# Seven half-size products for the left half of the output projection, with the weight sums made during the input projection

## The chip, the cores and the metric

The kernel runs on one core of a Trainium2 chip. The metric is the time in device microseconds, as the median of the runs. A profile shows five engines: PE (matrix multiplication, with its weight loads as PEld), DVE (vector), ACT (scalar, activations), POOL (here an issuer of transfers and some element work) and SP (an issuer of transfers).

## What is computed

One encoder layer for 512 positions and a width of 2048, everything in 32-bit floats. Cut to what matters:

```
h = x @ w_in                       # (512,2048) @ (2048,8192)
qa,ka,va,ga,qb,kb,vb,gb = split(h) # eight blocks of 1024 columns
ya = dilated_attention(qa,ka,va)   * silu(ga)      # 16 heads, group A
yb = neighbourhood_attention(qb,kb,vb) * silu(gb)  # 16 heads, group B
out = concat(ya, yb) @ w_out       # (512,2048) @ (2048,2048)
result = layer_norm(alpha * x + out, gain, bias)
```

Every matrix product is made three times over: each operand is split into a high part that is rounded to the matmul's format and a low part that is the rest, and the product is high x high + low x high + high x low. The high part is an ACT copy, the low part a DVE subtraction, so each weight tile of 128 x 1024 costs one ACT and one DVE instruction before PE can use all of it.

## The kernel before

The program has four stages.

*Early block* (`plain_block`, L268): the first four of sixteen gate column tiles, while x is loaded and its sums are formed.

*Projection blocks* (`strassen_block`, L351, run by `run_blocks`, L491). Six blocks (k, q and v of each group) and, after the fourth, one block for the next six gate column tiles (`MID`), are each made as seven products of half-size matrices instead of eight (Strassen's scheme in a form with few sums). A block is a row of *jobs*; a job is one weight tile, twelve 512-wide matmuls (L405 to L407; L395 to L397 for the gates, 256 wide). For each job there are up to four steps: DVE adds two weight tiles (L373), ACT rounds (L377), DVE subtracts (L382), PE multiplies. `run_blocks` writes out the order by hand: at position n it adds for job n+3, rounds for n+2, does what is queued "behind" n (evictions, loads, sums of results), subtracts for n+2 and multiplies for n. PE, DVE and ACT keep this order.

```
if 0 <= n + 3 < len(jobs): jobs[n + 3][0]()       # add (DVE)
if split_: h = jobs[n + 2][1]()                   # high (ACT)
for fn in behind.pop(n, ()): fn()                 # what was put behind n
if split_: ready.append(jobs[n + 2][2](h))        # low (DVE)
if 0 <= n < len(jobs): jobs[n][3](*ready.pop(0))  # matmuls (PE)
```

POOL meanwhile writes the attention bias tables to memory: `prep_heads` (L156) for the sixteen heads of group A, eight loads and one store a head (L161, L163) through the buffers b0 and b1 in turn, then `prep_b` (L165 on) for group B through the same two. Its order is left to a scheduler, but everything on POOL runs one after the other.

*Attention* (the loop at L845, 136 steps of 128 queries of one head, eight steps a pair of heads). Each step has scores (L677, L678), a minimum on DVE (L634), an exponential on ACT (L638), two steps later transposes on PE (L697), and every fourth step the product with v (L719). Between them `fill` issues matmuls of two kinds: the remaining six gate tiles (`gate_unit`, L566, 48 wide matmuls each), then the first half of K of the output projection (`out_first`, L788). How many are issued per step is a table (`amount`). The order is written out for PE, SP, DVE and ACT. `share` (L725) sends the softmax denominators out and back in rows through POOL; `gated` (L744) divides and splits y into halves as `yk`.

*Output.* For all four column blocks of 512 the second half of K is multiplied (L778); column blocks 0 and 1 first, then for each of the four row blocks of 128 the column blocks 2 and 3. alpha x is added (`residual`, L911), `finish` adds the sums and takes statistics, `norm` (L919) normalises a row block and writes it out; in two row blocks it uses ACT and POOL for one quarter. The last row block has its own `last_norm`, in which PE makes the shift rows.

Of the kernel before, what the change touches and what calls it, by code (L numbers as in the profile page):

```python
# [65 lines left out]
EARLY, MID = 4, 6  # L66
# [5 lines left out]
def hybrid_layer(tc, xT, xn, w_in, w_early, w_mid, w_gate, w_out, t5x, brow, rpb, cmask, eye, gain, lbias, out):  # L72
    nc = tc.nc
    from contextlib import ExitStack
    with ExitStack() as ctx:
# [59 lines left out]
        sg_d = dram.tile([2 * PAIRS, 128, S], F32, name="sg_d")  # L135
        rc_d = dram.tile([2 * PAIRS, 8, 128], F32, name="rc_d")
# [214 lines left out]
        def strassen_block(src, kind, g, hooks):  # L351

            base = len(jobs)
            units, tiles = 4, 2
            cols, wide = (128 * MID // 2, (512, HALF * (MID // 2 - 2))) if kind == "s" else (512, (512, 512))

            def load(q, tags):
                def run():
                    for u in range(units):
                        raw = slot(tags[u], F32, "braw")[:, :2 * cols]  # L360
# [6 lines left out]
            def product(i, pool, q, other=None, onto=None):  # L367
# [7 lines left out]
                def high(u):  # L375
                    h = halves.next("wh", F32R)[:, :2 * cols]
                    nc.scalar.activation(h, raws[q][u], AF.Copy)  # L377
                    return h

                def low(u, h):  # L380
                    l = halves.next("wl", F32R)[:, :2 * cols]
                    nc.vector.tensor_tensor(l, raws[q][u], f(h), ALU.subtract)  # L382
                    return h, l

                def run(u, h, l):
                    if u == 0 and first:
                        accs.extend(bank(pool, "acc")[:, :n] for n in wide)
                    if kind == "s":
                        for kk in range(2):
                            k = 2 * u + kk  # L390
                            ah, al = operand(i, k)
                            for n in range(MID // 2):
                                c = slice(cols * kk + 128 * n, cols * kk + 128 * n + 128)
                                o = accs[n // 2][:, HALF * (n % 2):HALF * (n % 2) + HALF]
                                nc.tensor.matmul(o, h[:, c], ah, start=first and k == 0 and n % 2 == 0, stop=False, skip_group_check=skip)  # L395
                                nc.tensor.matmul(o, h[:, c], al, start=False, stop=False, skip_group_check=skip)  # L396
                                nc.tensor.matmul(o, l[:, c], ah, start=False, stop=k == 7 and (n % 2 == 1 or n == MID // 2 - 1),  # L397
                                                 skip_group_check=skip)
# [25 lines left out]
            def pair(name):  # L424
                if name not in made:
                    t = temps.next(name)
                    made[name] = [t[:, :512], t[:, 512:512 + wide[1]]]
# [10 lines left out]
            for q, ahead, i in ((0, 6, 0), (1, 4, 1), (3, 2, 2)):  # L438
                behind.setdefault(base - ahead if base else -4, []).append(load(q, tags[i]))
            at(2, 2, load(2, tags[1]))  # L440
# [30 lines left out]
            def put(name, ch, half, t):  # L471
# [4 lines left out]
                sg = vst.next("sg")[:, :wide[t]]  # L476
                silu(sg, o)
                for n in range(wide[t] // HALF):
                    nc.sync.dma_start(sg_d[EARLY + MID // 2 * ch + 2 * t + n][:, HALF * half:HALF * half + HALF], sg[:, HALF * n:HALF * n + HALF])
# [44 lines left out]
        stream = [w_gate[i] for i in range(2 * (2 * PAIRS - EARLY - MID))] + [w_out[8 * dc + u] for dc in range(4) for u in range(4)]  # L524
# [10 lines left out]
        def prepare():  # L535
# [8 lines left out]
            if not raws:  # L544
                return
            raw = raws.pop(0)
# [197 lines left out]
        def gated(i):  # L744

            y = yt[i]
            t = slot(y_tags[i], F32R, "yk").rearrange("p (s q) -> p s q", s=2)
            yk.append(t)

            def divide():  # L750
                nc.vector.tensor_tensor(y, y, rcs[i], ALU.mult)
                later(0, high)

            def high():
                nc.scalar.activation(t[:, 0], y, AF.Copy, scale=0.5)
                hold(2, low)

            def low():
                nc.vector.scalar_tensor_tensor(t[:, 1], y, 0.5, f(t[:, 0]), op0=ALU.mult, op1=ALU.subtract)
# [8 lines left out]
        def out_load(ring, dc, u):  # L768
            return load_split(ring, w_out[dc * 8 + u])

        def out_mms(acc, t, u, wh, wl, first, last, part=slice(0, 512)):
            c = slice(t * 128, t * 128 + 128)
            for kk in range(2):
# [3 lines left out]
                for n, (s, w) in enumerate(((0, wh), (1, wh), (0, wl))):  # L777
                    nc.tensor.matmul(acc[:, part], yk[k][:, s, c], w[:, wk], start=first and kk == 0 and n == 0,  # L778
# [3 lines left out]
        def keep(t, to, acc):  # L782
            if t % 2:
                nc.vector.tensor_copy(to, acc)
            else:
                nc.scalar.activation(to, acc, AF.Copy)

        def out_first(dc):  # L788

            if dc % 2 == 0:  # L790
                for t in range(4):
                    z[t].append(slot(f"x{6 + 2 * t + dc // 2}", F32, f"z{t}").rearrange("p (s q) -> p s q", s=2))
            accs = []
            for u in range(4):
                wh, wl = next_weight()
                for t in range(4):
# [3 lines left out]
                    if u == 3:  # L800
                        later(0, lambda t=t: keep(t, z[t][dc // 2][:, dc % 2], accs[t]))

        def fillers():
            for j in range(EARLY + MID, 2 * PAIRS):
                yield from gate_unit(j)
            z.extend([] for _ in range(4))
            for dc in range(4):
# [17 lines left out]
        def close():  # L825

            for fn, dve in tasks.pop(step[0], ()):
                if dve and 0 <= step[0] < 134:
# [5 lines left out]
        load_kq(0)  # L834
        load_bias(0)
        load_v(0)
        engines = {mybir.EngineType.PE, mybir.EngineType.SP, mybir.EngineType.DVE, mybir.EngineType.Activation}
        with tc.manual_schedule(engines=engines):
            prepare()
            for _ in range(3):  # L840
                close()
            while step[0] < 0:
                fill(7)
                close()
            for n in range(136):  # L845
# [12 lines left out]
                if mixing:  # L858
                    if exponent:
                        exponent()  # L860
                    behind_min(2)
                    fill(2)
                    mine, theirs, y, t = values(n // 4 - 1)
                    nc.scalar.activation(t, theirs, AF.Copy)
                    nc.vector.tensor_tensor(y, mine, t, ALU.add)
                    fill(amount - 2)
                else:
                    fill(2)
                if 2 <= n < 130:
                    turn(n - 2)  # L870
                if b == 3 or n >= 134:
                    behind_min(99 if n >= 134 else 2 if len(held) > 3 and held[0][0] > 1 else 1)
# [6 lines left out]
                if n >= 8 and n % 8 == 1:  # L879
# [8 lines left out]
            for n in (0, 400):  # L888
                fill(n)
                while tasks or held:  # L890
                    behind_min(99)
                    close()
        z = [[zt[i // 2][:, i % 2] for i in range(4)] for zt in z]

        gb, bb = [], []
        for tiles, src, first in ((gb, gain, 0), (bb, lbias, 6)):
            for i in range(4):
                t = slot(f"n{first + i}", F32, "gain")
                nc.sync.dma_start(t, _view(src, 512 * i, [[0, 128], [1, 512]]))
                tiles.append(t)  # L900

        xl = {}

        def load_x(i):
            for t in range(4):
                if t % 2 == 0:
                    two = slot(f"s{t // 2}", F32, "xl").rearrange("p (t q) -> p t q", t=2)
                xl[t, i] = two[:, t % 2]
# [222 lines left out]
```

## Time and profile before

| what | value |
|---|---|
| median of the runs | 973.45 us (lowest 973.0) |
| the profiled execution | 973.54 us, span 971.8 us, granted clock 0.998 |
| PE busy | 963.0 us, 4861 matmuls |
| DVE busy | 768.5 us |
| ACT busy | 501.3 us |
| POOL busy | 181.6 us |
| moved | 194.18 MB, mean 200 GB/s |

The span is the time from the first to the last instruction of one profiled execution; the time of a run has a little more around it. The first job of the projection blocks starts at 50.0 us, the first scores at 595.9, the last product of the output ends near 962.6. A line of a timeline gives start and duration in us, the engine, the line of the kernel, the operation, what it writes and reads, and in brackets how long the engine stood idle before it and what ended that.

### The profile page before, as it was taken

To read this page: it belongs to the slowest core of one execution; us is meant where nothing else is said; L and a number is where in the kernel's file an instruction comes from. 1 tells how busy PE (TensorE), PEld (TensorE's weight loads), DVE (VectorE), ACT (ScalarE), POOL (GpSimd) and SP (SyncE) were. 2 spreads that over 40 slices of the span, in tenths; PEclk is the share of its full clock that TensorE was granted. 3 is DMA by queue.
4 is the path that set the end of the run, shared out by engine and by line. 5 is a ranking of instruction groups with operands and counts; after the bars stand their busy time and mean duration, and the time that the engine had idled before them with its cause. 6 is when DMAs were issued, how large, how long until landed. Compare 5 with 4: busy or idle time off the path is not lost.

```text
span 971.8 us, 14211 instructions
## 1 busy us (share of the span) xinstructions
PE 963.0 (99%) x4861; PEld 804.6 (83%) x4861; DVE 768.5 (79%) x1169; ACT 501.3 (52%) x870; POOL 181.6 (19%) x321
## 2 busy tenths in 40 slices
PE   8999999999999999999999999999999999999997
PEld 6878888888888889998888888888888888888886
DVE  7897778679789778789679875788877777777877
ACT  7454444444444344454445544777777776763300
POOL 1006646735645000000000000111111010010020
PEclk9999999999999999999999999999999999999999
DMA  9715797698496086272196178777787667678213
GB/s 331 283 65 133 224 332 213 169 313 219 115 348 200 37 255 159 74 278 92 44 294 180 48 227 279 245 228 246 242 276 221 214 210 228 197 238 287 73 58 116
DMA packets 121255, 194.18 MB, mean 200 GB/s; under 512 B 49551, under 2 KB 70415, under 8 KB 121184
## 3 DMA queue, kind: packets, MB, share of 16 engines
q1 hardware_dynamic: 108672, 170.21, 54.8%
q0 software_dynamic: 11936, 22.42, 8.3%
q8 instruction: 38, 0.62, 0.3%
q10 hardware_dynamic: 576, 0.66, 0.2%
q14 instruction: 33, 0.27, 0.1%
HBM read 148.69 MB, written 44.50 MB: 199 GB/s over the span
## 4 chain that ended last, share of the span: by engine, by line
PE 97%; DMA 1%; DVE 1%; ACT 0%; issue 0%; SPq 0%; DVEq 0%; ACTq 0%
PE acc L405 16%; PE acc L407 16%; PE acc L406 16%; PE acc L778 16%; PE acc L572 6%; PE pv L719 4%; PE pt L697 4%; PE sc L678 2%; PE sc L677 2%; PE acc L397 2%; PE acc L396 2%; PE acc L395 2%; PE pt L260 1%; PE acc L279 1%; PE sc L778 1%; PE acc L280 1%
## 5 line engine op out<-in xcount | busy, mean ns | idle before, releaser
L377 ACT ACTIVATE wh<-braw 128x1024 fp32r<-128x1024 f32 (+1 forms) x196 | 202.1, 1031 | 277.3 <-PE acc L406 202.4
L382 DVE TENSOR_TENSOR wl<-braw,wh 128x1024 fp32r<-128x1024 f32 (+1 forms) x196 | 234.3, 1197 | 57.9 <-ACT wh L377 57.6
L405 PE MATMUL acc<-wh,xk 128*128 128x512 f32 x384 | 151.3, 394 | 0.0
L407 PE MATMUL acc<-wl,xk 128*128 128x512 f32 x384 | 149.7, 390 | 0.0
L406 PE MATMUL acc<-wh,xk 128*128 128x512 f32 x384 | 149.5, 389 | 0.0
L373 DVE TENSOR_TENSOR braw<-braw 128x1024 f32<-128x1024 f32 (+1 forms) x112 | 132.4, 1182 | 0.0
L778 PE MATMUL acc<-wh,yk 128*128 128x512 f32 x320 | 113.5, 407 | 0.0
L405 PE MATMUL acc<-wh,op 128*128 128x512 f32 x288 | 113.1, 393 | 0.0
L407 PE MATMUL acc<-wl,op 128*128 128x512 f32 x288 | 112.2, 390 | 0.0
L406 PE MATMUL acc<-wh,op 128*128 128x512 f32 x288 | 112.1, 389 | 0.0
L703 DVE TENSOR_TENSOR tl<-pt,th 128x256 fp32r<-128x256 f32 (+1 forms) x128 | 71.1, 556 | 30.3 <-ACT th L702 28.5
L407 PEld LDWEIGHTS acc<-wl,xk 128*128 128x128 f32 x384 | 72.1, 188 | 15.3
L405 PEld LDWEIGHTS acc<-wh,xk 128*128 128x128 f32 x384 | 72.1, 188 | 15.2 <-ACT bias L151 0.9
L406 PEld LDWEIGHTS acc<-wh,xk 128*128 128x128 f32 x384 | 72.2, 188 | 14.4
L638 ACT ACTIVATE p<-s,mn 128x512 f32<-128x512 f32 (+1 forms) x96 | 62.4, 650 | 30.6 <-DVE mn L634 29.9
L634 DVE CUSTOM_DVE_ANT_0 s<-sc,biases 128x512 f32<-128x512 f32 (+2 forms) x128 | 67.6, 528 | 11.4 <-PE sc L678 11.0
L702 ACT ACTIVATE th<-pt 128x256 fp32r<-128x256 f32 (+1 forms) x128 | 62.2, 486 | 23.0 <-PE pt L697 21.3
L778 PEld LDWEIGHTS acc<-wh,yk 128*128 128x128 f32 x320 | 58.1, 189 | 8.4 <-ACT wh L88 0.4
L161 POOL DMA_DIRECT2D bias<-rows_d x128 | 61.4, 487 | 16.1 <-DMA rows_d<-bias 5.2
L407 PEld LDWEIGHTS acc<-wl,op 128*128 128x128 f32 x288 | 54.1, 188 | 11.4
L406 PEld LDWEIGHTS acc<-wh,op 128*128 128x128 f32 x288 | 54.1, 188 | 10.9
L405 PEld LDWEIGHTS acc<-wh,op 128*128 128x128 f32 x288 | 54.1, 188 | 10.9
(188 smaller groups left out, 1774.6 us busy)
## 6 DMA issues: line engine op xcount, KB each, us to landing
braw<-in_w_in SPq DMA_DIRECT2D x96, 512.0 KB
wraw<-in_w_out SPq DMA_DIRECT2D x32, 512.0 KB
k_d<-kst SPq DMA_DIRECT2D x64, 128.0 KB
q_d<-kst SPq DMA_DIRECT2D x64, 128.0 KB
v_d<-vst SPq DMA_DIRECT2D x32, 256.0 KB
q<-q_d SPq DMA_DIRECT2D x32, 256.0 KB
k<-k_d SPq DMA_DIRECT2D x16, 512.0 KB
braw<-in_w_mid SPq DMA_DIRECT2D x16, 384.0 KB
```

What stands on the lines that cost most here:

```text
L161: nc.gpsimd.dma_start(bt[16 * r:16 * r + 16], _view(rows_d, h * 16 * ROW + 463 - 64 * r, [[ROW - 1, 16], [1, 560]]))
L373: nc.vector.tensor_tensor(raws[q][u], raws[q][u], raws[other][u], ALU.add)
L377: nc.scalar.activation(h, raws[q][u], AF.Copy)
L382: nc.vector.tensor_tensor(l, raws[q][u], f(h), ALU.subtract)
L405: nc.tensor.matmul(accs[t], ah[:, q], h[:, c], start=first and k == 0, stop=False, skip_group_check=skip)
L406: nc.tensor.matmul(accs[t], al[:, q], h[:, c], start=False, stop=False, skip_group_check=skip)
L407: nc.tensor.matmul(accs[t], ah[:, q], l[:, c], start=False, stop=k == 7, skip_group_check=skip)
L634: nc.vector.tensor_tensor_reduce(*flat, bias, 1.0, 3e38, ALU.add, ALU.min, mn)
L638: nc.scalar.activation(p[:, to:to + n].rearrange("p (b r c) -> p b r c", r=8, c=c), s[:, :n].rearrange(order, r=8, c=c), AF.Exp, bias=mn, ...
L702: nc.scalar.activation(th, pt[:, :nch], AF.Copy)
L703: nc.vector.tensor_tensor(tl, pt[:, :nch], f(th), ALU.subtract)
L778: nc.tensor.matmul(acc[:, part], yk[k][:, s, c], w[:, wk], start=first and kk == 0 and n == 0, stop=last and kk == 1 and n == 2)
```

## The change

- `MID` is 4 instead of 6. The gate block has two tiles a side, so 14 jobs of 24 matmuls of 256 columns instead of 28 of 18, and two more `gate_unit`s run in attention.
- The left half of the output's columns (column blocks 0 and 1) is made by seven half-size products over all of K, after attention. The right half stays as it was: column blocks 2 and 3, first half of K in attention, second half after it, column block 2 for all rows (`second_half`) and column block 3 row block by row block (`third`, and the tail).
- The products need sums of weights: four sums for each of eight column strips. `sum_weights` makes them in the projection blocks: POOL loads four tiles of 128 x 512 into b0 and b1, DVE adds four times (L522), POOL stores each sum to `t_d`. It is placed behind the jobs 30, 39, 48, 142, 152, 162, 172 and 182, the additions four to seven positions later.
- They also need sums of y. POOL stores each y to `y_d` in attention (L784); after attention `again` loads it back, `combine_y` makes the sums, `high_y` and `low_y` split them.
- Results of column blocks 2 and 3 are added to alpha x as they are evicted (L811), x being loaded in attention. POOL's order is written out in attention too. The table of `amount` is ((4,5,3,5) if n < 80 else (4,4,3,4)) in place of ((3,5,3,5) if n < 76 else (5,6,4,6)), the loop has 132 steps, `share` comes one step later.
- The jobs after attention are run by `project`, with its order written out as in the blocks. `norm` is on DVE and one small ACT instruction alone.

The diff, cut to its core:

```diff
-EARLY, MID = 4, 6
+EARLY, MID = 4, 4
...
+        def sum_weights(n, u, kk):
+
+            c, two = slice(512 * kk, 512 * kk + 512), []
+
+            def load():
+                two.extend(slot(f"b{m}", F32, "wsum")[:, :1024].rearrange("p (s q) -> p s q", s=2) for m in range(2))
+                for m, q in enumerate((0, 8, 12, 4)):
+                    nc.gpsimd.dma_start(two[m // 2][:, m % 2], w_out[q + u][:, c])
+
+            def put(m):
+                a, b = two
+                o, p = ((a[:, 0], a[:, 1]), (a[:, 1], b[:, 0]), (b[:, 0], a[:, 0]), (b[:, 1], b[:, 0]))[m]
+                nc.vector.tensor_tensor(o, o, p, ALU.add)
+                nc.gpsimd.dma_start(t_d[m][u][:, c], o)
+
+            behind.setdefault(n, []).append(load)
+            for m in range(4):
+                behind.setdefault(n + 4 + m, []).append(lambda m=m: put(m))
...
+        for n, start in enumerate((30, 39, 48, 142, 152, 162, 172, 182)):
+            sum_weights(start, n // 2, n % 2)
         with tc.manual_schedule(engines={mybir.EngineType.PE, mybir.EngineType.DVE, mybir.EngineType.Activation}):
             run_blocks()
...
+        def project(n):
+
+            if n + 2 < len(jobs) and jobs[n + 2][0]:
+                h = jobs[n + 2][0]()
...
+                behind_min(99)
+            for fn in at_job.pop(n, ()):
+                fn()
+            if n + 2 < len(jobs):
+                ready_w.append(jobs[n + 2][1](h) if jobs[n + 2][0] else None)
+            if n >= 0:
+                jobs[n][2](ready_w.pop(0))
+                close()
...
+        p1 = product(1, pss, 0)
+        p2 = product(2, pst, 4)
+        o2 = second_half(2, 8)
+        product(6, None, 12, p1)
+        p5 = product(5, pst, 16)
+        product(7, None, 20, p1)
+        p3 = product(3, pacc, 24)
+        for t in range(2):
+            jobs.extend(((None, None, lambda w, t=t: third(t)), (None, None, lambda w: None)))
...
+        product(4, None, 32, p1)
...
+        at(34, lambda: done(3, 0, accs3[0]), lambda: norm(0))
+        at(36, lambda: done(3, 1, accs3[1]), lambda: norm(1))
...
-                amount = ((3, 5, 3, 5) if n < 76 else (5, 6, 4, 6))[b]
+                amount = ((4, 5, 3, 5) if n < 80 else (4, 4, 3, 4))[b]
```

How the instructions stand now, at the three places of which the prediction speaks. First DVE in the second projection block, around jobs 36 and 37. A row is the line, the operation, what is written and read, and the size; braw are weight tiles, wl their low halves, wsum the tiles of the new sums, kst a staging tile of results. Before:

```order
L382 TENSOR_TENSOR wl<-braw,wh 128x1024
L373 TENSOR_TENSOR braw<-braw 128x1024
L89 TENSOR_TENSOR kst<-pt,kst 128x512
L382 TENSOR_TENSOR wl<-braw,wh 128x1024
L373 TENSOR_TENSOR braw<-braw 128x1024
L382 TENSOR_TENSOR wl<-braw,wh 128x1024
L373 TENSOR_TENSOR braw<-braw 128x1024
```

and with the change, where the fourth and fifth rows are job 35's low half and job 37's addition, as in the rows before:

```order
L383 TENSOR_TENSOR wl<-braw,wh 128x1024
L374 TENSOR_TENSOR braw<-braw 128x1024
L89 TENSOR_TENSOR kst<-pt,kst 128x512
L383 TENSOR_TENSOR wl<-braw,wh 128x1024
L374 TENSOR_TENSOR braw<-braw 128x1024
L522 TENSOR_TENSOR wsum<-wsum 128x512
L383 TENSOR_TENSOR wl<-braw,wh 128x1024
L374 TENSOR_TENSOR braw<-braw 128x1024
L522 TENSOR_TENSOR wsum<-wsum 128x512
```

The first addition of weights stands between job 37's addition and job 36's low half; the next follow one job apart.

Second, POOL from the bias tables of the last heads of group A on (rows_d and biasa_d hold those tables, rpbs and gt belong to group B). Before:

```order
L161 DMA bias<-rows_d 16x560 x16
L163 DMA biasa_d<-bias 128x560 x2
L174 DMA rpbs<-in_cmask 128x144
L176 DMA rpbs<-in_rpb 8x15x48 x16
L183 ISA
L183 TENSOR_TENSOR gt<-rpbs 128x360
```

and with the change:

```order
L163 DMA bias<-rows_d 16x560 x16
L165 DMA biasa_d<-bias 128x560 x2
L517 DMA wsum<-in_w_out 128x512 x4
L523 DMA t_d<-wsum 128x512 x3
L517 DMA wsum<-in_w_out 128x512 x2
L523 DMA t_d<-wsum 128x512
L517 DMA wsum<-in_w_out 128x512 x2
L523 DMA t_d<-wsum 128x512 x3
L517 DMA wsum<-in_w_out 128x512 x2
L523 DMA t_d<-wsum 128x512
L517 DMA wsum<-in_w_out 128x512 x2
L523 DMA t_d<-wsum 128x512 x4
```

The loads and stores of the first three strips stand behind all sixteen heads' tables and ahead of group B's.

Third, the end, with the change alone. PE, from the column-3 jobs on (wlast are column 3's weights, the L919 rows product 4, the 256-wide rows and the last three row block 3 and what follows it):

```order
L804 MATMUL acc<-wlast,yk 128x512 x48
L919 MATMUL acc<-wh,yk 128x512 x2
L804 MATMUL acc<-wlast,yk 128x512 x24
L804 MATMUL acc<-wlast,yk 128x256 x20
L919 MATMUL acc<-wl,yk 128x512
L919 MATMUL acc<-wh,yk 128x512 x2
```

and DVE, from the closing of row block 1 (its norm is the L1050 and L1054 rows, the last two low halves of product 4 the L898 row, the L1040 row the first half of row block 3):

```order
L1054 SCALAR_TENSOR_TENSOR z_7236<-z_7236,rs,gain 128x512
L1050 SCALAR_TENSOR_TENSOR z_7236<-z_7236,mv,gain 128x512
L1040 TENSOR_TENSOR z_7238<-acc,z_7238 128x256
L1054 SCALAR_TENSOR_TENSOR z_7236<-z_7236,rs,gain 128x512
L898 TENSOR_TENSOR wl<-lraw,wh 128x1024 x2
L1041 BN_STATS st_5089<-z_7238 128x6
```

The norms of the first two row blocks stand on DVE ahead of the low halves that product 4 needs, and PE has row block 2 and a part of row block 3 between product 4's first matmuls and the rest.

More of the change, by code (lines that the diff above doesn't have):

```diff
@@ L353, in strassen_block @@
             base = len(jobs)
-            units, tiles = 4, 2
-            cols, wide = (128 * MID // 2, (512, HALF * (MID // 2 - 2))) if kind == "s" else (512, (512, 512))
+            units, tiles = (2, 1) if kind == "s" else (4, 2)
             def load(q, tags):
@@ L475, in put @@
                     return
[L476 removed]
+                sg = vst.next("sg")[:, :512]
                 silu(sg, o)
[L478 to L479 removed]
+                for n in range(2):
+                    nc.sync.dma_start(sg_d[EARLY + 2 * ch + n][:, HALF * half:HALF * half + HALF], sg[:, HALF * n:HALF * n + HALF])
             for t in range(tiles):
@@ new lines, in product, with run @@
+        def product(i, pool, m0, upon=None):
+            accs = [] if upon is None else upon
+            first, skip = upon is None, upon is not None
+            def run(w, u):
+                if u == 0 and first:
+                    accs.extend(bank(pool, "acc") for _ in range(2))
+                for t in range(2):
+                    for kk in range(2):
+                        k = 2 * u + kk
+                        ah, al = factor(i, k)
+                        c = slice(512 * kk, 512 * kk + 512)
+                        m = slice(128 * t, 128 * t + 128)
+                        for n, (a, b) in enumerate(((ah, w[0]), (al, w[0]), (ah, w[1]))):
+                            nc.tensor.matmul(accs[t], a[:, m], b[:, c], start=first and k == 0 and n == 0, stop=n == 2 and k == 7,
+                                             skip_group_check=skip)
+            for u in range(4):
+                jobs.append((*convert(m0 + u), lambda w, u=u: run(w, u)))
+            return accs
@@ new lines, in second_half, with run, first @@
+        def second_half(dc, m0):
+            accs, now = [], []
+            def run(w, u, ts):
+                for t in ts:
+                    if u == 4:
+                        accs.append(bank(pacc, "acc"))
+                    for _ in out_mms(accs[t], t, u, *w, u == 4, u == 7):
+                        pass
+            def first(w, u):
+                now[:] = [w]
+                run(w, u, (0, 1))
+            for u in range(4, 8):
+                jobs.append((*convert(m0 + u - 4), lambda w, u=u: first(w, u)))
+                jobs.append((None, None, lambda w, u=u: run(now[0], u, (2, 3))))
+            return accs
@@ new lines, in copy, with gains @@
+        def copy(name, tag, t, acc):
+            if name not in parts:
+                two = slot(tag, F32, "part")[:, :1024].rearrange("p (s q) -> p s q", s=2)
+                parts[name] = [two[:, 0], two[:, 1]]
+            nc.scalar.activation(parts[name][t], acc[t], AF.Copy)
+        def gains():
+            for tiles, src, first in ((gb, gain, 0), (bb, lbias, 4)):
+                for i in range(4):
+                    t = slot(f"n{first + i}", F32, "gain")
+                    nc.sync.dma_start(t, _view(src, 512 * i, [[0, 128], [1, 512]]))
+                    tiles.append(t)
@@ L886, in hybrid_layer @@
                     gated(i - 1)
-                close()
[L888 to L900, printed above, removed]
@@ new lines, in hybrid_layer @@
+        for t in (2, 3):
+            acc = bank(pacc, "acc")
+            cuts = (slice(0, 256), slice(256, 512)) if t == 3 else (slice(0, 512),)
+            accs = [acc] if len(cuts) == 1 else [acc, bank(pss, "sc")]
+            for o, part in zip(accs, cuts):
+                for u in range(4, 8):
+                    list(out_mms(o, t, u, *wts[u], u == 4, u == 7, part))
+            if t == 3:
+                idle = bank(pss, "sc")
+                for _ in range(AWAKE):
+                    nc.tensor.matmul(idle, yk[8][:, 0, 0, 0:128], wts[4][0][:, 0:512], start=True, stop=True)
+            with tc.manual_schedule(engines={mybir.EngineType.DVE}):
+                if t == 2:
+                    home("t7", 0, 2, 3)
+                    for m in range(2):
+                        put(0, m + 2, p1[m])
+                        stats(0, m + 2)
+                    nc.vector.tensor_tensor(z[3][0], z[3][0], gb[0], ALU.mult)
+                for m, part in enumerate(cuts):
+                    finish(3, t, accs[m], part, 3 + m)
+                if t < 3:
+                    norm(t)
+                else:
+                    last_norm(rows)
```

363 lines of the change are left out of this document (216 added, 147 removed).

## Prediction

> **What bounds the kernel now.** I read the page's busy table first, then the chain of waits, then the busy table by stretches.
>
> ```profile
> span 971.8 us, 14211 instructions
> PE 963.0 (99%) x4861; PEld 804.6 (83%) x4861; DVE 768.5 (79%) x1169; ACT 501.3 (52%) x870; POOL 181.6 (19%) x321
> PE 97%; DMA 1%; DVE 1%; ACT 0%; issue 0%; SPq 0%; DVEq 0%; ACTq 0%
> ```
>
> ```profile
> 50.00:583.00 533.00, 533.00 (x2645) 450.27 (x2645) 431.41 (x450) 246.15 (x293) 143.93 (x254) 1.00 0.60 183
> ...
> 658.06:675.27 17.21, 17.21 (x95) 14.11 (x93) 14.67 (x33) 13.60 (x32) 2.14 (x4) 1.00 0.73 231
> 675.27:689.83 14.56, 14.56 (x87) 12.04 (x86) 11.20 (x32) 10.48 (x30) 1.57 (x3) 1.00 0.82 268
> ```
>
> (The second fence's columns: stretch, length, then busy time and count of PE, weight load, DVE, ACT and POOL, the clock, the DMA share and GB/s.) PE is busy throughout, and the chain is PE for 97%. So a matmul taken away is worth its issue interval, and a wait of PE is paid in full. PE's busy means (390 ns) overlap and are not that interval; runs without a gap in the chain give it:
>
> ```profile
> 902.49 2.72 PE sc L778 x12
> ...
> 959.76 2.89 PE sc L778 x24
> ```
>
> The first is twelve 512-wide matmuls: 2.72 / 12 = 0.227 us. The second is 24 of 256: 2.89 / 24 = 0.120 us.
>
> **The arithmetic removed.** The middle gate block goes from 7 products x 8 K tiles x 3 column tiles x 3 = 504 half-wide matmuls to 336: 168 x 0.120 = 20.2 us less. Two more gate units of 48 wide matmuls: 96 x 0.227 = 21.8 us more. The left half of the output goes from 384 wide matmuls to 7 x 8 x 2 x 3 = 336: 48 x 0.227 = 10.9 us less. Sum: **-9.3 us**, about 1%. Everything else decides the sign.
>
> **The first weight sum.** The change puts 32 additions (L522) into DVE's written order, four for each of eight column strips, on tiles that POOL loads. The first addition stands, as the order shows, behind the addition for job 37 and ahead of the low half of job 36's weights. In the trace of before that place is here:
>
> ```profile
> 148.76 1.22 DVE L382 TENSOR_TENSOR wl<-braw,wh 128x1024 fp32r<-128x1024 f32 x1
> 149.90 1.23 DVE L373 TENSOR_TENSOR braw<-braw 128x1024 f32<-128x1024 f32 x1
> 151.03 1.23 DVE L382 TENSOR_TENSOR wl<-braw,wh 128x1024 fp32r<-128x1024 f32 x1
> ```
>
> ```profile
> 153.84 0.39 PE L405 MATMUL acc<-wh,xk 128*128 128x512 f32 x1
> 154.06 0.39 PE L406 MATMUL acc<-wh,xk 128*128 128x512 f32 x1
> 154.29 0.39 PE L407 MATMUL acc<-wl,xk 128*128 128x512 f32 x1
> ```
>
> DVE comes to it at 151.0. PE starts job 36 at 153.84 and at 154.29 needs the low half (wl) that is queued behind the addition. Up to this place nothing ahead of it has changed, so these times hold for the new kernel. When do the tiles arrive? Their loads (L517) stand in POOL's order behind all sixteen heads' bias tables, and they use b0 and b1, the buffers those tables go through. POOL in the trace of before:
>
> ```profile
> 88.39 7.80 POOL L161 DMA_DIRECT2D bias<-rows_d  x16 [5.17 <-DMA rows_d<-bias]
> ...
> 98.86 7.80 POOL L161 DMA_DIRECT2D bias<-rows_d  x16
> ...
> 158.52 4.40 POOL L161 DMA_DIRECT2D bias<-rows_d  x9 [0.57 <-DMA biasa_d<-bias]
> ...
> 189.42 0.58 POOL L163 DMA_DIRECT2D biasa_d<-bias  x1
> 191.67 0.57 POOL L163 DMA_DIRECT2D biasa_d<-bias  x1 [1.67 <-DMA bias<-rows_d]
> 192.74 0.54 POOL L174 DMA_DIRECT2D rpbs<-in_cmask  x1 [0.50 <-DMA biasa_d<-bias]
> ```
>
> Two heads cost 16 loads of 0.49 us and the landings; POOL's chain runs from 88.39 to 191.67 whatever PE does, and nobody waits for it until attention. L174 at 192.74 is the first instruction to reuse b0; the new loads take its place. The addition needs the first two: issued at 192.7 and 193.3, landed some 2.9 us after issue, by the nearest rows:
>
> ```profile
> biasa_d<-bias POOLq DMA_DIRECT2D x16, 280.0 KB, 2.9
> ...
> sg_d<-sgo POOLq DMA_DIRECT2D x6, 256.0 KB, 2.9
> ...
> DMA to landing us min/median/max: 2.8/4.7/7.9
> ```
>
> (The last row is of the rc reload, POOL's slowest kind.) So 196.2, plus the addition (0.6 from start to the next start) and the low half (1.2): PE goes on at 198.0, **43.7 us** after 154.29. Two bounds. With PE still, the load queue empties, and three pairs of heads from 158.52 on could go at the pace of the first, 98.86 - 88.39 = 10.5 us, instead of 34.2 / 3 = 11.4: 2.8 us sooner, 40.9. If the loads land in 7.9, 48.7. I take half of the first effect: **42.3**. All of DVE's work behind it (job 36 and on) is late by as much, and PE with it. ACT has nothing to give meanwhile: it rounds job 38's weights only after DVE has summed them.
>
> When PE returns its clock counts too:
>
> ```profile
> 1.32 2.74 PE L125 MATMUL sc<-calm 128*128 128x512 bf16 x6 [1.32 <-POOL calm L122]
> ...
> 962.70:967.20 4.50, 3.24 (x13) 1.87 (x11) 3.93 (x11) 0.56 (x2) 0.00 (x0) 1.00 0.00 0
> 967.30:971.80 4.50, 0.00 (x0) 0.00 (x0) 1.26 (x3) 0.00 (x0) 0.00 (x0) 0.50 0.64 233
> ```
>
> The first six matmuls, as wide as the 0.227 ones, take 2.74 / 6 = 0.46 us each, and after the last matmul the clock reads 0.50. No gap inside the trace is long enough to show a restart, so the bounds are 0 and a repeat of the start: six at 0.46 instead of 0.227, 1.4 us. I take **1.4**, the start being the nearest row. DVE has also lost its lead of two jobs and needs 1.14 + 1.14 + 0.6 = 2.9 us for each of the next three jobs against PE's 2.72: **0.5**. [...]
>
> The second and third strips (jobs 39 and 48) follow on POOL: their buffers are free when the first stores have landed (last addition near 204, store 0.6 + 2.9, loads 1.1 + 2.9: 212), and DVE comes to their additions one job ahead of job 43, near 216. No wait, with 4 us to spare. The other five strips are ten jobs (27 us) apart, ahead of a POOL that has long finished its tables. Their 20 additions of 0.6 us lie in DVE's free 19% of the blocks (431.4 of 533).
>
> **Into attention.** The last strip's four additions come after the blocks' last evictions, and the first bias load must wait until their stores have left b0.
>
> ```profile
> 589.90 0.69 DVE L224 TENSOR_TENSOR vst<-w,vst 128x512 fp32r<-128x512 f32 x1
> ...
> 590.73 0.61 SPq L661 DMA_DIRECT2D biases<-biasa_d  x1
> ...
> 596.60 0.69 DVE L634 CUSTOM_DVE_ANT_0 s<-sc,biases 128x512 f32<-128x512 f32 x1 [6.01 <-PE sc L678]
> ...
> 599.58 0.60 PE L697 MATMUL pt<-ident,p 128*128 128x128 f32 x4
> ```
>
> In this frame: additions from 590.5, the second stored by 592.3, landed 595.2; bias load 595.3 instead of 590.7, landed by 599; softmax 2.4 us late of 596.6. PE needs its result at 599.58; DVE and ACT take 1.7 us in between, so **1.2** (0 to 4).
>
> **Attention.** Matmuls per eight steps go from 32 to 34 up to step 79, then 30 in place of 42. Thirty make a group A stretch 17.21 - 2 x 0.227 = 16.8 us against DVE's 14.67 plus about 0.5 for evictions that now add x: 90%. PE still sets it; **0.5**, between 0 and 6 (1 us in each of six stretches).
>
> **The tail.** In the order, the norms of row blocks 0 and 1 stand ahead of product 4's low halves.
>
> ```profile
> 952.94 0.27 DVE L933 BATCH_NORM_AGGREGATE mv<-st 128x2 f32<-128x24 f32 x1
> ...
> 956.93 0.69 DVE L916 TENSOR_TENSOR z<-acc,z 128x512 f32<-128x512 f32 x1
> ...
> 959.46 0.74 DVE L930 SCALAR_TENSOR_TENSOR z<-z,rs,gain 128x512 f32<-128x512 f32 x1
> ...
> 962.68 0.42 DVE L916 TENSOR_TENSOR z<-sc,z 128x256 f32<-128x256 f32 x1 [1.21 <-PE sc L778]
> ...
> 966.37 2.18 DVE L985 SCALAR_TENSOR_TENSOR z<-z,rs,acc 128x512 f32<-128x512 f32 x4
> ```
>
> A norm on DVE alone is 952.94 to 960.2 less two foreign rows of 0.6: 6.1 us. Let T be the start of the column-3 jobs. PE: 48 + 2 matmuls (T+11.3), row block 2 and most of half of row block 3 (24 x 0.227 + 20 x 0.120, T+19.2), then 24 of product 4 and the half's end (T+25.2), then it needs job 38's low half. DVE: block 0 closed and normed T+5.5 to T+12.9, two low halves T+15.2 (in time), block 1 closed and normed up to a row that reads row block 3's half (T+25.2), one more pass, the low half at T+27.6: PE waits **2.4** (0 to 6). Then PE ends at T+35.5. DVE gets product 4's sums at T+32.7 and has 10 rows (5.6 us), then norm(2)'s eight passes of 0.66 mixed with the last block's six: T+47.5, so 12.0 us behind PE's last block instead of 968.55 - 962.65 = 5.9: **+6.1** (2 to 8). The loads there (28 weight tiles and 8 of y at 0.5 MB, x and the gains at 2 MB each) are 22 MB in 36 jobs of 2.72 us, 225 GB/s; the attention row above moved 268.
>
> **Sum.** 971.8 - 9.3 + 42.3 + 1.4 + 0.5 + 1.2 + 0.5 + 2.4 + 6.1 = 1016.9 us of span. The profiled run took 973.54 with a span of 971.8, 1.7 more, and the median is 973.45: **1018.6 us**.
>
> **Rivals.**
> - *The first sum doesn't wait.* If the tiles were there at 151, what is left is -9.3 + 1.2 + 0.5 + 8.5 = +0.9: 974.4, no slower than before; with the tail hidden too, 966. It needs POOL's tables 40 us sooner; the pair pace of 10.5 against 11.4 leaves no room for that. Chance 0.07.
> - *Each early strip waits.* If POOL's stores and loads take 4.7 to 7.9 instead of 2.9, the 4 us of room at job 43 goes, and the second and third strips each hold DVE for some 8 us: 1035. For it: the queue refills after the stop, and the DMA share is high there. Chance 0.08.
> - *Attention becomes DVE's.* At 30 matmuls DVE's 90% may queue ahead of the transposes; 2 us in each of six stretches: 1030. Against it: DVE's group B stretches have 3 us free (11.20 of 14.56). Chance 0.05.
> - The forecast: 0.80, by itself 1008 to 1030.
>
> The low end is the stop at 40.9 with nothing for restart, transition, attention and tail, 971.8 - 9.3 + 40.9 + 1.7 = 1005; the high end, 1034, reaches to the second rival. A measurement of this kernel tells 2% (19.5 us) from no change. Faster by more than that needs under 954, which no sum here reaches: 0.01; within it the first rival: 0.07; slower: 0.92.
>
> **What would show it.** PE's largest wait should be one of about 42 us near 154, its releaser DVE's wl, DVE's own idle time there ended by the DMA into wsum, and POOL's first L517 near 192. The clock should read 0.5 there for some microseconds. Attention stretches of 30 should be near 16.8 and 14.1 us. From PE's last projection matmul to the end should be 15, not 9.1 us. If DVE's first L522 starts near 151, the forecast is wrong by 40 us.

## The result, and the profile after

The changed kernel takes 1063.27 us (median of four runs, 1056.81 to 1064.29), the kernel before 973.43 beside it: a ratio of 1.0911 (95% interval 1.0856 to 1.0965). The ratio leaves out one of the four runs of the kernel before, a slow one of 1199.3 us. Slower, as forecast, but by 90 us where 45 were predicted, and above the 1034 to which the range went. The profiled execution has a span of 1062.3 us against 971.8. First the page:

```profile
span 1062.3 us, 14230 instructions
PE 974.8 (92%) x4741; PEld 803.2 (76%) x4741; DVE 806.9 (76%) x1230; ACT 516.7 (49%) x889; POOL 220.1 (21%) x399
```

PE was busy for 99% of the span and is now for 92%. To see where it isn't, add up for all pairs of neighbouring matmuls the distance between their starts beyond the first one's interval (0.227 us for a width of 512, 0.120 for 256; 0.10 for 192 and 0.07 for 128 are estimates from starts that lie 0.09 to 0.18 and 0.03 to 0.11 us apart in the trace of before). This holds both stops and time lost while the clock read 0.50 (in the change matmuls of 512 then start 0.43 us apart):

| PE's lost time, us | before | after | difference |
|---|---|---|---|
| blocks, up to attention's first scores | 11.2 | 53.5 | +42.3 |
| attention, to its last scores | 21.7 | 63.1 | +41.4 |
| output and end | 1.9 | 17.8 | +15.9 |
| span less lost time | 936.9 | 927.9 | -9.0 |

The arithmetic came out as worked out (-9.3 predicted). Of the blocks' 42.3, 39.2 lie at the stop (between 150 and 215 us) and 2.0 in the first 50 us. These 2.0 are scatter: the changed kernel and its variants below, whose code is the same up to there, lose between 2.8 and 5.9 us in that time, each in its profiled execution.

The three losses have names in PE's waits (columns: total, times, longest):

```profile
PE acc L407 <- DVE wl L383: 38.2, 1, 38.2
PE pv L747 <- DVE mn L662: 8.1, 1, 8.1
PE sc L705 <- DVE mn L662: 8.0, 2, 6.2
PE sc L705 <- DVE y L1140: 7.8, 2, 4.3
PE acc L919 <- DVE wl L898: 4.9, 7, 2.3
PE pt L1219 <- DVE nms L1217: 4.8, 1, 4.8
PE pt L725 <- ACT tmp L760: 4.0, 8, 0.5
```

The releaser of the first six is DVE. A wait for an engine that is itself waiting has to be followed one step on, to DVE's own waits:

```profile
DVE wsum L522 <- DMA wsum<-in_w_out: 41.2, 2, 40.5
DVE y L1140 <- DMA y_d<-y: 10.6, 2, 5.4
DVE s L662 <- DMA biases<-biasa_d: 9.4, 1, 9.4
DVE z L811 <- DMA xl<-in_xn: 9.4, 2, 7.5
```

Four transfers. The first is the forecast's. Here is its place, DVE, then POOL, then PE:

```profile
151.02 1.22 DVE L374 TENSOR_TENSOR braw<-braw 128x1024 f32<-128x1024 f32 x1
192.78 0.69 DVE L522 TENSOR_TENSOR wsum<-wsum 128x512 f32<-128x512 f32 x1 [40.54 <-DMA wsum<-in_w_out]
193.39 1.22 DVE L383 TENSOR_TENSOR wl<-braw,wh 128x1024 fp32r<-128x1024 f32 x1
```

```profile
187.64 0.57 POOL L165 DMA_DIRECT2D biasa_d<-bias  x1 [1.40 <-DMA bias<-rows_d]
188.36 1.07 POOL L517 DMA_DIRECT2D wsum<-in_w_out  x2 [0.15 <-issue]
```

```profile
156.07 0.39 PE L406 MATMUL acc<-wh,xk 128*128 128x512 f32 x1
194.66 0.79 PE L407 MATMUL acc<-wl,xk 128*128 128x512 f32 x1 [38.21 <-DVE wl L383]
195.26 0.63 PE L405 MATMUL acc<-wh,xk 128*128 128x512 f32 x1
...
198.66 0.39 PE L407 MATMUL acc<-wl,xk 128*128 128x512 f32 x1
198.89 0.40 PE L405 MATMUL acc<-wh,xk 128*128 128x512 f32 x1
```

DVE comes to the addition at 152 and gets its tiles at 192.7, 4.4 us after POOL's first load, which POOL issues as soon as it has left the tables. For nine matmuls after the stop PE's starts are 0.43 us apart instead of 0.227.

Of the other three, the sum had the first at 1.2 us, and the last two not at all. The bias load of attention's first head waits for the last strip's second store, which holds b0 (POOL, SP, DVE):

```profile
616.23 0.54 POOL L523 DMA_DIRECT2D t_d<-wsum  x1 [0.80 <-DVE wsum L522]
```

```profile
623.59 2.76 SPq L689 DMA_DIRECT2D biases<-biasa_d  x2
```

```profile
626.68 0.69 DVE L662 CUSTOM_DVE_ANT_0 s<-sc,biases 128x512 f32<-128x512 f32 x1 [9.41 <-DMA biases<-biasa_d]
```

Twice DVE can't write y (L1140), because one of y's two buffers, n5 and n7, is still being stored; the store (L784) stands in POOL's order right behind the reload of the reciprocals (L763):

```profile
685.96 1.06 POOL L763 DMA_DIRECT2D rc<-rc_d  x2 [1.78 <-DMA rc_d<-tmp]
687.01 0.57 POOL L784 DMA_DIRECT2D y_d<-y  x1
```

```profile
694.81 0.68 DVE L1140 TENSOR_TENSOR y<-pv,tmp 64x512 f32<-64x512 f32 x1 [5.35 <-DMA y_d<-y]
```

And the x of columns 2 and 3 is fetched too late; the fourth load is issued after DVE has begun to wait for it:

```profile
861.31 0.43 SPq L816 DMA_DIRECT2D xl<-in_xn  x1
```

```profile
867.48 0.69 DVE L811 SCALAR_TENSOR_TENSOR z<-xl,acc 128x512 f32<-128x512 f32 x1 [7.50 <-DMA xl<-in_xn]
```

DVE waits from 859.98 (867.48 - 7.50).

### The profile page after: what moved, and what is told of

The parts are those of the page before. It is cut to its first block, busy times and chain, and to the rows that moved or that the text cites. A ratio compares the mean times of both kernels' runs of the same rounds, so it can differ in the third digit from the quotient of the medians.

```text
span 1062.3 us, 14230 instructions
## 1 busy us (share of the span) xinstructions
PE 974.8 (92%) x4741; PEld 803.2 (76%) x4741; DVE 806.9 (76%) x1230; ACT 516.7 (49%) x889; POOL 220.1 (21%) x399
## 5 line engine op out<-in xcount | busy, mean ns | idle before, releaser
L378 ACT ACTIVATE wh<-braw 128x1024 fp32r<-128x1024 f32 x182 | 193.2, 1062 | 309.5 <-PE acc L406 193.6
L383 DVE TENSOR_TENSOR wl<-braw,wh 128x1024 fp32r<-128x1024 f32 x182 | 223.9, 1231 | 42.7 <-ACT wh L378 42.5
L407 PE MATMUL acc<-wl,xk 128*128 128x512 f32 x384 | 150.6, 392 | 38.2 <-DVE wl L383 38.2
L374 DVE TENSOR_TENSOR braw<-braw 128x1024 f32<-128x1024 f32 x104 | 128.2, 1233 | 0.1
L407 PEld LDWEIGHTS acc<-wl,xk 128*128 128x128 f32 x384 | 72.6, 189 | 54.0 <-DVE wl L383 38.6
L407 PE MATMUL acc<-wl,op 128*128 128x512 f32 x288 | 112.2, 390 | 0.0
L406 PEld LDWEIGHTS acc<-wh,xk 128*128 128x128 f32 x384 | 72.6, 189 | 14.6
L600 PE MATMUL acc<-xk,wh 128*128 128x512 f32 x256 | 81.8, 411 | 0.0
L804 PE MATMUL acc<-wh,yk 128*128 128x512 f32 x192 | 68.8, 409 | 0.0
L523 POOL DMA_DIRECT2D t_d<-wsum x32 | 17.4, 544 | 234.4 <-DVE wsum L522 218.7
L407 PEld LDWEIGHTS acc<-wl,op 128*128 128x128 f32 x288 | 54.1, 188 | 11.4
L406 PEld LDWEIGHTS acc<-wh,op 128*128 128x128 f32 x288 | 54.1, 188 | 11.0
```

The costliest lines, as they stand in the source:

```text
L374: nc.vector.tensor_tensor(raws[q][u], raws[q][u], raws[other][u], ALU.add)
L406: nc.tensor.matmul(accs[t], al[:, q], h[:, c], start=False, stop=False, skip_group_check=skip)
L407: nc.tensor.matmul(accs[t], ah[:, q], l[:, c], start=False, stop=k == 7, skip_group_check=skip)
L600: nc.tensor.matmul(acc, w[:, k * 128:k * 128 + 128], X[8 * u + k][:, s], start=u == 0 and n == 0 and k == 0, stop=u == 1 and n == 2 and k ...
L804: nc.tensor.matmul(acc[:, part], yk[k][:, t // 2, s, c], w[:, wk], start=first and kk == 0 and n == 0, stop=last and kk == 1 and n == 2)
```

## The experiments

Times are medians; the change itself is 1063.3. Theory: every one of these waits is an order or a buffer, and goes when that alone is altered. Rivals stand with each run.

**The stop at 156 us.** Two edits of the change, one to the place of the strips, one to the engine of the additions.

```diff
-        for n, start in enumerate((30, 39, 48, 142, 152, 162, 172, 182)):
+        for n, start in enumerate((112, 122, 132, 142, 152, 162, 172, 182)):
```

> The first three strips of weight sums start at jobs 112, 122 and 132 instead of 30, 39 and 48, behind both groups of bias tables; the other five stay where they are, and so does the work. Theory (the stop at 156 us is DVE's first addition waiting for POOL's loads, which stand behind the sixteen heads' tables): the stop of 38.4 us and the 2.0 us of half clock behind it are gone, 1063 - 40 = 1023 us, and no wait of PE for L383's wl above 5 us is left. Rival (the strips hold up POOL's and DVE's order wherever they stand, or b0 and b1 are as scarce there): the wait moves to job 116 and the time stays at 1050 or more. The other gaps (620, 691, 816, 860, 1035 us of the old time axis) stay as they are under both.

Measured 1020.1, 43 us less, of which the traces put 39.2 at the stop and 2.3 in the first 50 us. L407 is no longer among PE's twelve longest waits, and the other gaps are where they were. The rival is out.

```diff
-                nc.vector.tensor_tensor(o, o, p, ALU.add)
+                nc.gpsimd.tensor_tensor(o, o, p, ALU.add)
```

> The change with the strips where it has them (30, 39, 48, 142, ...), and its 32 additions of weights done by POOL, in its own order behind its own loads, instead of by DVE; nothing else. Theory (what costs 40 us is not that the tiles come late, which they still do, but that DVE's in-order queue stands behind the addition that waits for them): PE's stop at 156 us is gone though POOL's first L517 is still near 192, 1063 - 40 = 1023 us; a few us more if POOL's slower passes (its 128x512 multiplication took 1.54 us in the kernel before) bring the last strip later to attention. Rival 1 (the first strip's tiles or the product behind them are what PE waits for): no change, 1060. Rival 2 (POOL's passes hold up the bias tables and DVE): 1040 or more.

Measured 1015.7. POOL comes to its loads no sooner, and its first addition is at 200:

```profile
192.40 1.07 POOL L517 DMA_DIRECT2D wsum<-in_w_out  x2 [0.26 <-DMA biasa_d<-bias]
...
199.97 1.28 POOL L522 TENSOR_TENSOR wsum<-wsum 128x512 f32<-128x512 f32 x1
```

```profile
PE acc L407 <- DVE wl L383: 3.1, 3, 1.4
```

So the late tiles cost little by themselves (between 215 us and attention PE loses 8.7 us here, 4.2 in the change). What cost 40 us was that everything else DVE does stood behind them. It is lower than the first experiment because POOL, which nobody holds to the jobs' pace, makes its last sum at 550, so that the wait at attention's start goes too.

**Into attention.**

```diff
-        for n, start in enumerate((30, 39, 48, 142, 152, 162, 172, 182)):
+        for n, start in enumerate((112, 121, 130, 139, 148, 157, 166, 175)):
```

> All eight strips start at jobs 112, 121, ... 175, nine apart, so that the last strip's additions end seven jobs ahead of attention. Theory (the gap of 6.4 us at 620 and 2.7 us of half clock are the last strip's stores, which must land before the bias load may use b0): on top of the first experiment another 9 us, 1014. Rival (the first bias load is late for another reason, a backlog of the blocks' last stores): as the first experiment, 1023, with softmax's wait for the biases still near 9 us.

Measured 1012.4, 7.8 below the first experiment. What is left of PE's waits for softmax's minimum at scores is

```profile
PE sc L705 <- DVE mn L662: 1.2, 1, 1.2
```

against 6.2 for the longest. The rival is out; a new gap of 2.4 us appeared at 515, where an addition and the reload of x's right half (xback) now meet on DVE.

**The store of y.** Three edits: no store, another queue, another place of the reload ahead of it.

```diff
-                nc.gpsimd.dma_start(y_d[i % PAIRS][:, i // PAIRS], yt[i])
...
-            nc.sync.dma_start(cut_y[i].rearrange("p n q -> p (n q)"), y_d[i].rearrange("p n q -> p (n q)"))
+            nc.sync.dma_start(cut_y[i].rearrange("p n q -> p (n q)"), w_out[i])
```

> The 16 stores of y to DRAM are left out, and the reload of y reads as many bytes of the output weights instead; so the left half of the output is not the reference's. Everything else is the changed kernel. Theory (the gaps at 691 and 816 us are y's two buffers, held until the store has landed): both gaps of 4.5 and 3.6 us and their 2.6 and 1.6 us of half clock go, 1063 - 12 = 1051, and DVE's wait for y_d at L1140 is gone. Rival (the store is only what is last: the reload of the reciprocals on the same queue would keep DVE late anyway): less than 4 us, 1059 or more.

Measured 1048.7, 14.6 less; both gaps are gone.

```diff
-                nc.gpsimd.dma_start(y_d[i % PAIRS][:, i // PAIRS], yt[i])
+                nc.sync.dma_start(y_d[i % PAIRS][:, i // PAIRS], yt[i])
```

> The 16 stores of y go out from SP's queue instead of POOL's; nothing else. Theory (the store is late because it stands behind the reload of the reciprocals on POOL's queue): both gaps of PE behind DVE's L1140 go as they did where the store was left out, 1063 - 14 = 1049. Rival 1 (the DMA engines are loaded there, whichever queue issues): the gaps stay, 1060 or more. Rival 2 (SP's loads of biases, k and q now wait behind the store, which waits for ACT and DVE): slower than 1063.

Measured 1050.2, 13.1 less: the same bytes in the same steps through SP cost nearly nothing, so neither the bytes nor the load on the DMA engines was enough to cause the waits. Both rivals are out. Not separated is how POOL's order delays the store: in the change the first late one is issued 1.7 us after y is ready (687.0 and 685.3), and both also take longer than the rest to land.

```diff
-                if n >= 8 and n % 8 == 2:
+                if n >= 8 and n % 8 == 1:
                     share(i - 1)
```

> The reciprocals' step (share) goes back from n%8==2 to n%8==1, as in the kernel before; nothing else. In the trace of the change the two y stores that landed late (issued at 687.0 and 809.8 us, landed 7.8 and 9.5 later) stand in POOL's order right behind the reload of the reciprocals (L763); the others landed in 2.3 to 3.1. Theory (that reload is what delays the store): the eight waits of transposes for ACT's tmp (4.0 us in all) go, and the stores land some 2 us sooner, so each of the two gaps is about 2 us shorter: 1063 - 4 - 4 to 8 = 1051 to 1055. Rival (the store is late through the load on the DMA engines, not through what stands ahead of it): only the 4 us of the transposes, 1059.

Measured 1079.0: 15.7 **more**, and neither theory nor rival had that sign. The order on POOL explains it. In the change thirteen stores were issued just ahead of the reciprocals' store and reload, two right behind, and the last one has none near it. One step earlier, the reload overtakes the thirteen too:

```profile
705.37 1.06 POOL L763 DMA_DIRECT2D rc<-rc_d  x2 [1.36 <-DMA rc_d<-tmp]
706.43 0.57 POOL L784 DMA_DIRECT2D y_d<-y  x1
```

From issue to landing of the y store, first in the change, then here, and what PE waits for:

```profile
DMA to landing us min/median/max: 2.3/3.1/9.1
```

```profile
DMA to landing us min/median/max: 3.0/6.5/9.6
```

```profile
PE sc L705 <- DVE y L1140: 25.2, 10, 4.2
```

The mechanism of the theory held in the main (behind the reload the store is issued later and lands later): DVE's waits for it go from 2 to 11, and from 10.6 to 39.9 us. The sign failed because I looked only at the two late stores and not at what the edit would do to the other thirteen. I had also misread the landings: apart from the two late stores they take 2.3 to 6.6 us in the change, 3.1 being the median of all sixteen; and here some stores right behind the reload land in 3.0 to 3.6. So the place on the queue shifts the landing, but doesn't settle it alone.

**The loads of x.**

```diff
-                if n >= 92 and n % 4 == 0 and n < 108:
-                    load_x((n - 92) // 4)
+                if n >= 84 and n % 4 == 0 and n < 100:
+                    load_x((n - 84) // 4)
```

> The four loads of x for the columns 2 and 3 are issued at steps 84 to 96 instead of 92 to 104; nothing else is changed. Theory (the gaps at 856 and 860 us are DVE waiting at L811 for x, whose last load was issued at 861.3 us, after it was wanted): both gaps (1.9 and 8.3 us) and 3.1 us of half clock go, 1063 - 13 = 1050. Rival (the DMA share of 0.95 there makes any load late, and the loads now collide with others): half of it or less, 1057 or more, with the wait moved to the biases or to k and q.

Measured 1049.1, 14.2 less, with no wait of L811 for x left.

**The tail.**

```diff
-        at(36, lambda: done(3, 1, accs3[1]), lambda: norm(1))
+        at(36, lambda: done(3, 1, accs3[1]))
+        at(37, lambda: norm(1))
```

> The norm of row block 1 moves one job later (37 instead of 36), behind the low half for job 38 in DVE's order; nothing else. Theory (PE's gap of 2.47 us at 1035 and 1.7 us of half clock are job 38's low half standing behind that norm, and DVE sits idle for 4.2 us just after): 1063 - 4 = 1059, and the low half for job 38 is done near 1029. Rival (DVE's chain after PE's end is what sets the end, and takes the same time more): no change, 1063.

Measured 1058.4, 4.9 less. The gap shrank to 1.4 us, and its half clock went: in the profiled executions the output loses 2.9 us less. Another 2.3 lie in the first 50 us and are scatter.

**Together.** The strips nine apart, x earlier, y stores on SP, and share at n%8==1; then with the tail's edit; then that with share back at 2; then that with two passes taken off DVE at the end.

> Strips from job 112 on, nine apart; loads of x 8 steps earlier; y stores on SP's queue; share at n%8==1. Theory (the waits are separate and add up): 1012.4 (the strips alone) - 14 (x) - 14 (y) - 4 (share) = 980, within 2% of the kernel before. Rival (what one wait frees, the next takes up: DVE or the DMA engines set attention at 30 matmuls per eight steps): 995 or more, with new waits for biases, k or q between 680 and 850 us.

Measured 984.7, ratio to before 1.0118 (1.0103 to 1.0134): the theory, 5 us over its number.

> The four edits together (strips from job 112 nine apart, x 8 steps earlier, y stores on SP's queue, share at n%8==1) and the norm of row block 1 one job later. Theory (the edits add up): 984.7 - 5 = 980. Rival (the tail is DVE's by now, since the waits ahead of it are gone and its loads come no sooner): 984 or more.

Measured 982.8, ratio 1.0100 (1.0085 to 1.0115). Nearer the rival: the tail's edit gives 1.9 here, and 0.7 in the output of the profiled executions. In the fourfold kernel the same 2.47 us gap had cost no clock (below), so there was less to gain.

> As the five edits together, but share stays at n%8==2, as in the change. Theory (with the y store on SP's queue the share's place only decides whether transposes wait 8 times 0.5 us for ACT's tmp, or twice for den): 980 + 4 - 2 = 982. Rival (the share at step 1 crowds ACT and DVE, as the single edit suggested that took 16 us more): 976 or less.

Measured 991.8: 9 us more, where 2 were expected and the rival said less than 976. The edit that cost 16 us with the store on POOL gains 9 once the store is on SP. Of the 9, the profile's waits name

```profile
PE pt L725 <- ACT tmp L760: 4.5, 9, 0.5
PE pt L725 <- DVE tl L731: 1.9, 3, 0.7
```

and neither is among the waits with share at 1. The starts of PE's matmuls show the rest: these twelve transposes begin 0.65 to 0.82 us late, 8.4 us in all, and with share at 1 none is over 0.3 late. So the theory had the right place and too small a price: share at n%8==2 costs some 9 us and not 4.

```diff
+            if t == 2:
+                nc.vector.scalar_tensor_tensor(nm, mv[:, 0:1], -1.0, rs, op0=ALU.mult, op1=ALU.mult)
+                zt = z[t][0]
+                nc.scalar.activation(zt, zt, AF.Identity, bias=nm, scale=rs)
+                nc.gpsimd.tensor_tensor(zt, zt, gb[0], ALU.mult)
+                nc.gpsimd.tensor_tensor(zt, zt, bb[0], ALU.add)
...
-            for i in (0, 2, 3):
+            for i in (2, 3) if t == 2 else (0, 2, 3):
```

> As the run before (share at n%8==2), and in the norm of row block 2 the first column's two passes go from DVE to ACT (one) and POOL (two). Theory (the end is DVE's queue behind PE's last block): two passes of 0.7 us less, 982 - 1.4 = 980.6. Rival (POOL's two passes of 1.6 us, and the store behind them, become the last): no change or slower.

Measured 995.7, 3.9 more. The rival's outcome, though not by its mechanism: POOL's two passes (983.1 to 986.4) don't end last, but two of DVE's go slower beside them, and the last block's shift (nms), for which PE waits, is 1.4 us later (6.2 against 4.8). The two rows:

```profile
983.34 1.22 DVE L1223 SCALAR_TENSOR_TENSOR nm<-mv,rs 128x1 f32<-128x1 f32 x1
...
985.15 1.75 DVE L1050 SCALAR_TENSOR_TENSOR z<-z,mv,gain 128x512 f32<-128x512 f32 x1
```

In the fivefold kernel the first takes 0.15 us and the second 0.75; the pass between them keeps its 0.74. Some 1.6 of the 3.9 us lie at the start of the profiled execution and have nothing to do with the edit.

So five edits to orders and queues take back 80 of the 90 us. No version beats the kernel before. In the fivefold kernel PE's lost time is 53.3 us against 34.9, 18.4 more for 9.0 of arithmetic saved: 13.8 of it in the output and at the end, 3.1 in the blocks, 1.6 in attention.

```profile
span 981.2 us, 14247 instructions
...
PE 958.5 (98%) x4741; PEld 793.1 (81%) x4741; DVE 804.1 (82%) x1230; ACT 517.0 (53%) x889; POOL 211.3 (22%) x383
```

```profile
PE pt L1220 <- DVE nms L1218: 4.8, 1, 4.8
PE acc L919 <- DVE wl L898: 4.2, 5, 1.4
PE acc L407 <- DVE wl L383: 2.3, 1, 2.3
```

## Why the prediction was right about the first stop and wrong about attention

- **What bounds it; arithmetic (-9.3).** Right: -9.0.
- **The first weight sum (42.3, with restart and lost lead 44.2).** The mechanism was right in each step: the place in DVE's order, POOL behind the tables, the buffers, PE's wait for wl. Measured 38.4 + 2.0 of half clock = 40.4 in the trace, 43.1 in the first experiment, some 2 of them the scatter at the start. The stop alone fell under my lower bound of 40.9, for two reasons. PE came to job 36 2.0 us later than in the trace of before, through a longer stop at 7.3 us and half clock from 10.9 on; I should not have taken those times to the tenth. And POOL left the tables at 188.4 and not 192.7: it was 1.2 us ahead when PE stopped (157.3 against 158.5) and gained 3.1 in the stop, where I had taken 1.4 and at most 2.8. The loads then landed 3.5 us after issue, not 2.9. (The reload of rc, from which I took 7.9, isn't POOL's slowest kind: its median is 4.7 us, that of the stores of group B's tables from 128 KB tiles 5.3.)
- **Restart (1.4) and lost lead (0.5).** 2.0 for the two. But I charged the clock once. It was halved again after five of the shorter stops, from 625.3, 693.6, 819.9, 864.2 and 1038.3 us on.
- **Into attention (1.2, bounds 0 to 4).** This step failed in size: 6.4 + 2.7 of half clock = 9.1, and 7.8 by experiment, where a new gap of 2.4 came in. I had the right chain but let the last additions follow at 590.5 in the old frame, with stores landing 2.9 us after issue. POOL issued the last two loads of that strip only at 608.5, they landed 6.5 and 7.4 us later, DVE made the last three additions from 615.1 on, and the store issued at 616.2 let go of b0 at 623.5, 7.3 us later. From 616.0 to 623.5 the DMA engines were busy for 98% and moved 339 GB/s; I had taken landing times without asking for that load.
- **Attention (0.5, bounds 0 to 6).** This is the step that failed, and it cost most: +41.4 with the transition, 32 without. I looked at DVE's busy share and found, rightly, that PE still sets the pace: in the fivefold kernel the three group A stretches of eight steps at 30 matmuls take 16.7, 17.9 and 16.6 us (16.8 predicted), and the two of group B 14.5 and 15.1 (14.1 predicted). What I left out is that the change gives attention 16 new stores and four new loads, each with a deadline, and moves a step of the order. y's stores: 4.5 + 3.6 and 4.2 of half clock = 12.3 (13.1 and 14.6 by experiment). x's loads: 1.9 + 8.3 and 3.1 = 13.3 (14.2). share a step later: eleven transposes that begin 0.65 to 0.83 us late, 7.7 (8.9 by experiment, with y's stores on SP); the waits above name only 4.0 of it and 1.9 more for tl. Together 33.3, which accounts for the 32. The first two could be read from the order ahead of the run: in two places of sixteen y's store stands behind the reload in POOL's order, and DVE comes to write the same buffer 2.5 and 4.3 us after the issue; the fourth x is fetched at step 104 and used there.
- **The tail (2.4 + 6.1).** Right where it was worked out: the gap is 2.5 us (with 1.7 of half clock), and from PE's last projection matmul to the end it takes 14.6, with 15 predicted. Not in the sum were six more waits of products for low halves (3.6 us by the starts of the matmuls) and one for y (0.9); some 2 us of the stage's 15.9 are in smaller pieces.
- **Rivals.** DVE had only two waits at L522, of 40.5 and 0.7, so the early strips behind the first don't wait. Attention isn't DVE's. The first sum does wait. All three are out, but so is the claim that the list was complete: the forecast's 0.80 went to one story with one big term, and the other waits had no place in it.

## What to carry to other kernels

When a change puts a new transfer into a tuned in-order program, write down for each one its queue, what stands ahead of it there, and the instruction that first needs its data or its buffer; a busy share says nothing of such a deadline. An engine that takes on a side job in its written order lends its whole queue to that job's slowest input (40.5 us here), and an engine that nobody waits for can do the same job late at a much smaller cost (1015.7 us with POOL adding, 1063.3 with DVE). And test an edit on all instances that it moves: the step that was to help two stores put thirteen others behind the reload, and it changed its sign once another edit was in.

## What the runs showed of the hardware

In the trace of the change the clock was halved seven times before 1050 us: from 10.91, 161.09, 625.30, 693.57, 819.86, 864.24 and 1038.32 us on, for 3.41, 37.55, 6.83, 6.83, 3.41, 10.24 and 3.41 us. Each of these lengths is a whole multiple of the shortest.

The same short stop cost clock in one trace and not in another. The stop of 2.47 us in the tail (PE idle for 2.31) stands in nine of the traces. In the change PE is idle from 1035.73 to 1038.04, and the clock is halved from 1038.32 on; in the fourfold kernel PE is idle for the same time from 956.23 to 958.54, and behind it the clock reads 1.00. The two kernels differ in four edits, so what makes the difference isn't shown. (Columns as in the prediction: stretch, length, busy of PE, PEld, DVE, ACT, POOL, clock, DMA share, GB/s.)

```profile
1038.40:1041.60 3.20, 3.20 (x9) 2.54 (x8) 1.06 (x2) 0.00 (x0) 0.00 (x0) 0.50 0.01 2
```

```profile
958.80:962.00 3.20, 3.20 (x15) 2.63 (x15) 1.16 (x2) 0.00 (x0) 0.00 (x0) 1.00 0.04 13
```

Nine matmuls against fifteen in the same time. After the change's stops of 3.6 to 8.3 us the clock was halved for 3.41 to 10.24 us, 1.6 to 3.1 us of time each.

Beside POOL's passes two of DVE's took longer in the last experiment (1.22 and 1.75 us, against 0.15 and 0.75 in the fivefold kernel). With the 32 additions on POOL, over half of DVE's sums and low halves that overlap one took longer (23 of 40 took 1.48 to 2.39 us, the others 1.2 to 1.3). Eight passes that overlap one and read a matmul's result kept their 0.7.

```profile
224.49 1.21 DVE L374 TENSOR_TENSOR braw<-braw 128x1024 f32<-128x1024 f32 x1
...
226.22 1.72 DVE L383 TENSOR_TENSOR wl<-braw,wh 128x1024 fp32r<-128x1024 f32 x1
227.86 2.37 DVE L374 TENSOR_TENSOR braw<-braw 128x1024 f32<-128x1024 f32 x1
```

```profile
L383 DVE TENSOR_TENSOR wl<-braw,wh 128x1024 fp32r<-128x1024 f32 x182 | 232.9, 1283 | 44.6 <-ACT wh L378 44.4
```

The L383 group took 223.9 us in the change and L374 128.2; here they take 232.9 and 138.9. That is 19.7 us more over 32 additions, 0.6 us each, about what an addition costs DVE when it does it itself (0.61 from its start at 192.78 to the next at 193.39 in the change): the work was moved, the time on DVE wasn't saved, only the waiting.
